# A sliding-window matmul on one core: loading the fp32 weights by hardware DMA in 8 KB rows and casting them on VectorE

## The chip, the cores and the metric

The kernel runs on one core of one Trainium2 chip. The metric is device time in microseconds (us), lower is better. A profile of one execution goes with each kernel. Its span (first to last instruction) is 1.5 to 2 us shorter than the time of the run.

## The reference

```python
B, S, D, W = 4, 4096, 4096, 64      # x: [4, 4096, 4096] fp32, w: [4096, 4096] fp32
for b in range(B):
    o = int(offsets[b])             # known only at run time
    results.append(x[b, o:o+W] @ w) # [64, 4096] @ [4096, 4096]
```

So four windows of 64 rows, 256 rows in all, are multiplied by one big matrix. w is 67.1 MB and is read once. The windows of x are four times 1 MB. The output is 4.2 MB.

## The kernel before

The four windows are laid into two tiles of 128 partitions (two windows of 64 rows in each), transposed on TensorE, and used as stationary operands. w streams through in four groups of 1024 columns. GpSimd issues nearly all loads as software DMAs, which cast fp32 to fp16 on the way, 4 KB of each row of w at a time (1024 columns of fp32): on the page each of these loads of w writes 256.0 KB for 512 KB read.

```python
NG = 1024
wh_pool = ctx.enter_context(tc.tile_pool(name="wh", bufs=36))     # fp16 w tiles
xpair = [x_pool.tile([P, D], fp16, name=f"xpair{g}") for g in range(G)]
# ... three early loads by hardware DMA, eight by software DMA, then x:
for b in range(B):
    g, m = divmod(b, 2)
    nc.gpsimd.dma_start(                                   # casts to fp16
        out=xpair[g][m * WIN : (m + 1) * WIN, :],          # 64 partitions
        in_=x[b][bass.ds(off_vals[b], WIN), :],
    )
# ... then all other w tiles, by nc.gpsimd.dma_start(out=w_tile(ng, ki)[:], in_=w_src(ng, ki))
for ng in range(n_ng):                                     # 4 column groups
    for ki in range(n_full):
        for g in range(G):
            for j in range(n_sub):
                nc.tensor.matmul(out=acc[g][:, j * NT : (j + 1) * NT],
                                 lhsT=xT[g][:, ki * KT : (ki + 1) * KT],
                                 rhs=whk[:, j * NT : (j + 1) * NT], ...)
    # ... copy PSUM out, store
```

## Time and profile before

| | before |
|---|---|
| time, median of 3 runs | 188.69 us (188.68 to 189.26) |
| span of the profile | 187.1 us |
| PE / VectorE / ScalarE busy | 131.8 / 14.2 / 8.5 us |
| DMA | 9 tenths or more in all slices but the first and the last |
| HBM read / written | 71.30 / 4.19 MB |

These lines are from the page of the kernel before. PE is TensorE's matmuls, PEld its weight loads, DVE is VectorE, ACT ScalarE and POOL GpSimd. PE's line gives busy time, share of the span and instructions. The DMA and GB/s lines cut the span into 40 equal slices: the busy share of the DMA engines in tenths, and what they moved. GB/s counts the bytes written, so a load that casts to fp16 counts half of what it reads (the packets on the page come to 40.72 MB, for 71.30 MB read and 4.19 MB written in HBM).

```profile
span 187.1 us, 1496 instructions
PE 131.8 (70%) x576; PEld 54.8 (29%) x576; DVE 14.2 (8%) x13; ACT 8.5 (5%) x9; POOL 71.6 (38%) x140
...
DMA  4999999999999999999999999999999999999993
GB/s 147 291 205 218 215 205 209 210 209 210 210 208 210 262 209 262 208 209 209 210 209 209 209 210 210 209 209 210 210 209 208 211 208 210 209 209 210 258 416 154
...
HBM read 71.30 MB, written 4.19 MB: 403 GB/s over the span
```

The next lines are three pieces of the chain of waits (start in us, length in us, what). Each piece is one round of eight software loads: the ninth is issued when the first has landed.

```profile
82.21 9.48 DMA wh<-in_w_dram
...
92.23 9.50 DMA wh<-in_w_dram
...
102.26 9.48 DMA wh<-in_w_dram
```

From 92.23 to 102.26 is 10.03 us; over several rounds it is 10.02 us for eight loads of 524,288 bytes of fp32, so 418.5 GB/s are read. That is where the time goes: 75.5 MB at 418.5 GB/s would take 180.4 of the 187.1 us. PE waits for w again and again (22.5 us in all), and is not the limit.

These are GpSimd's issues of w loads from about 21 us on, each held until one of the four x loads had landed (columns: start, length, engine, line, operation, and in brackets the idle time before and what ended it).

```profile
21.10 0.53 POOL L112 DMA_DIRECT2D wh<-in_w_dram  x1 [1.97 <-DMA xpair<-in_x_dram]
...
23.53 0.53 POOL L112 DMA_DIRECT2D wh<-in_w_dram  x1 [1.90 <-DMA xpair<-in_x_dram]
25.93 0.53 POOL L112 DMA_DIRECT2D wh<-in_w_dram  x1 [1.88 <-DMA xpair<-in_x_dram]
...
28.37 0.53 POOL L112 DMA_DIRECT2D wh<-in_w_dram  x1 [1.92 <-DMA xpair<-in_x_dram]
```

One x load lands every 2.4 us. Each reads 1.05 MB, so x is read at about 430 GB/s, at full rate, and written as fp16 into 64 partitions at half of that, about 215 GB/s. (That is by the landings. The DMA's own count from 18.6 to 28.4 us is 210 GB/s written.)

### The profile page before, as it was taken

Reading aid. Unit: us, or ns where it says so; the run is one execution under the profiler, and the core shown is the slowest. Engines: PE = TensorE matmul, PEld = TensorE weight load, DVE = VectorE, ACT = ScalarE, POOL = GpSimd, SP = SyncE. Lnnn points to the kernel's source line nnn. Section 1 sums busy time; section 2 is a strip of 40 time slices with the busy share of each in tenths; the row PEclk is TensorE's granted clock in tenths of the full one; section 3 lists DMA queues with packets and bytes.
Section 4 is the critical chain, followed back from the end, with each engine's and each line's share of the span. In section 5 each row is a group of like instructions: output and inputs, shape, how many; then the busy total and the mean of one; then the engine's idle time right before and its main releaser. Section 6 shows DMA issues by size and latency. Waiting matters only on the chain.

```text
span 187.1 us, 1496 instructions
## 1 busy us (share of the span) xinstructions
PE 131.8 (70%) x576; PEld 54.8 (29%) x576; DVE 14.2 (8%) x13; ACT 8.5 (5%) x9; POOL 71.6 (38%) x140
## 2 busy tenths in 40 slices
PE   0000079999999585988888888888888888888820
PEld 0000076444444232333322322332233233323300
DVE  0000079100000020000002000000020000000020
ACT  2420000000002000000002000000020000000020
POOL 7343224343343242444344434434443426344200
PEclk9999999999999999699999999999999999999996
DMA  4999999999999999999999999999999999999993
GB/s 147 291 205 218 215 205 209 210 209 210 210 208 210 262 209 262 208 209 209 210 209 209 209 210 210 209 209 210 210 209 208 211 208 210 209 209 210 258 416 154
DMA packets 20344, 40.72 MB, mean 218 GB/s; under 512 B 2290, under 2 KB 2546, under 8 KB 20082
## 3 DMA queue, kind: packets, MB, share of 16 engines
q0 software_dynamic: 19040, 36.97, 102.2%
q1 hardware_dynamic: 866, 2.36, 3.3%
q10 hardware_dynamic: 432, 1.31, 2.1%
q8 instruction: 4, 0.07, 0.1%
q14 instruction: 2, 0.02, 0.0%
HBM read 71.30 MB, written 4.19 MB: 403 GB/s over the span
## 4 chain that ended last, share of the span: by engine, by line
DMA 64%; PE 17%; issue 7%; DVE 3%; POOL 3%; POOLq 1%; ACT 0%
DMA wh<-in_w_dram 57%; PE ps L146 16%; DMA xpair<-in_x_dram 6%; DVE xT L132 3%; POOL wh L74 2%; POOLq L83 1%; POOL wh L112 1%; PE ps L125 1%; PE ps L175 1%; DVE sth L188 0%; ACT sth L187 0%; POOLq L112 0%; POOL identity masks.py:197 0%; POOLq L94 0%; POOL xpair L94 0%
## 5 line engine op out<-in xcount | busy, mean ns | idle before, releaser
L146 PE MATMUL ps<-wh,xT 128*128 128x512 f16 x508 | 125.2, 382 | 22.6 <-DMA wh<-in_w_dram 22.5
L112 POOL DMA_DIRECT2D wh<-in_w_dram x116 | 61.2, 528 | 92.6 <-DMA wh<-in_w_dram 74.7
L146 PEld LDWEIGHTS <-xT 128*128 128x128 f16 x508 | 49.3, 97 | 98.2 <-issue 47.8
L125 PE MATMUL ps<-identity,xpair 128*128 128x128 f16 x64 | 5.5, 265 | 24.7 <-DMA xpair<-in_x_dram 24.7
L125 PEld LDWEIGHTS <-xpair 128*128 128x128 f16 x64 | 5.1, 123 | 24.9 <-issue 24.9
L132 DVE CAST xT<-ps 128x1024 f16<-128x1024 f32 x8 | 9.1, 1213 | 24.4 <-PE ps L125 24.4
L165 DVE COPY stage<-ps 128x1024 f32<-128x1024 f32 x2 | 2.4, 1224 | 70.9 <-PE ps L146 70.9
L164 ACT COPY stage<-ps 128x1024 f32<-128x1024 f32 x2 | 2.0, 1012 | 79.0 <-PE ps L146 79.0
L74 POOL DMA_DIRECT2D wh<-in_w_dram x8 | 4.4, 586 | 0.8 <-POOLq L211 0.8
L188 DVE COPY sth<-ps 128x512 f32<-128x512 f32 x2 | 1.4, 692 | 38.5 <-PE ps L175 38.5
L94 POOL DMA_DIRECT2D xpair<-in_x_dram x4 | 2.1, 519 | 5.7 <-DMA wh<-in_w_dram 5.7
L160 DVE COPY stage<-ps 128x1024 f32<-128x1024 f32 x1 | 1.2, 1223 | 32.2 <-DMA out_dram<-stage 32.2
L167 POOL DMA_DIRECT2D out_dram<-stage x4 | 2.1, 533 | 3.1 <-DMA wh<-in_w_dram 3.1
L79 ACT CAST wh<-w 128x1024 f16<-128x1024 f32 x3 | 3.0, 1043 | 4.7 <-DMA w<-in_w_dram 4.7
L159 ACT COPY stage<-ps 128x1024 f32<-128x1024 f32 x1 | 1.0, 1012 | 47.3 <-PE ps L146 47.3
L187 ACT COPY sth<-ps 128x512 f32<-128x512 f32 x2 | 1.2, 586 | 38.9 <-PE ps L175 38.9
L175 PE MATMUL ps<-whl,xT 128*128 128x512 f16 x4 | 1.3, 378 | 0.5 <-ACT sth L187 0.5
L107 POOL DMA_DIRECT2D whl<-in_w_dram x2 | 1.1, 528 | 1.3 <-DMA wh<-in_w_dram 1.3
L79 ACT ACT_TABLE_LOAD x1 | 1.3, 1283 | 1.3 <-PEq L211 1.3
L175 PEld LDWEIGHTS <-xT 128*128 128x128 f16 x4 | 0.4, 97 | 1.1 <-issue 0.4
masks.py:199 POOL TENSOR_SCALAR_AFFINE_SELECT identity<-identity 128x128 f16<-128x128 f16 x1 | 0.3, 287 | 0.1
masks.py:197 POOL MEMSET identity<- 128x128 f16 x1 | 0.3, 295 | 0.0
(4 smaller groups left out, 0.4 us busy)
## 6 DMA issues: line engine op xcount, KB each, us to landing
wh<-in_w_dram POOLq DMA_DIRECT2D x124, 256.0 KB, 9.5
xpair<-in_x_dram POOLq DMA_DIRECT2D x4, 512.0 KB, 12.7
out_dram<-stage POOLq DMA_DIRECT2D x4, 512.0 KB, 8.3
w<-in_w_dram SPq DMA_DIRECT2D x2, 512.0 KB, 6.4
out_dram<-sth SPq DMA_DIRECT2D x3, 256.0 KB, 5.6
w<-in_w_dram ACTq DMA_DIRECT2D x1, 512.0 KB, 4.3
out_dram<-stage SPq DMA_DIRECT2D x1, 512.0 KB, 7.0
out_dram<-stage ACTq DMA_DIRECT2D x1, 512.0 KB, 7.1
```

The lines of the kernel that those rows point to most:

```text
L74: nc.gpsimd.dma_start(out=w_tile(0, ki)[:], in_=w_src(0, ki))
L79: nc.scalar.copy(out=w_tile(0, k)[:], in_=w32[k][:])
L83: nc.values_load(off_i32[0:1, 2 * b : 2 * b + 1], engines=[POOL], min_val=0, max_val=S - WIN,)
L94: nc.gpsimd.dma_start(out=xpair[g][m * WIN : (m + 1) * WIN, :], in_=x[b][bass.ds(off_vals[b], WIN), :],)
L112: nc.gpsimd.dma_start(out=w_tile(ng, ki)[:], in_=w_src(ng, ki))
L125: nc.tensor.matmul(out=ps[t][:, q * KT : (q + 1) * KT], lhsT=xpair[g][:, k * KT : (k + 1) * KT], rhs=identity[:], start=True, stop=True,)
L132: nc.vector.tensor_copy(out=xT[g][:, t * NG : (t + 1) * NG], in_=ps[t][:])
L146: nc.tensor.matmul(out=acc[g][:, j * NT : (j + 1) * NT], lhsT=xT[g][:, ki * KT : (ki + 1) * KT], rhs=whk[:, j * NT : (j + 1) * NT], start= ...
L164: nc.scalar.copy(out=stage[(ng, 0)][:], in_=acc[0][:])
L165: nc.vector.tensor_copy(out=stage[(ng, 1)][:], in_=acc[1][:])
L167: nc.gpsimd.dma_start(out=out[2 * g : 2 * g + 2, :, cs : cs + NG], in_=stage[(ng, g)][:],)
L175: nc.tensor.matmul(out=acc[g][:, j * NT : (j + 1) * NT], lhsT=xT[g][:, ki * KT : (ki + 1) * KT], rhs=wlast[j][:], start=False, stop=True,)
```

## The change

The intent: no software DMAs at all. w is loaded as fp32 by the sync engine's hardware DMAs in 1 MB pieces with rows of 8 KB, and cast to fp16 on VectorE, which is nearly idle. Two column groups of 2048 take the place of four of 1024. The hardware loads of this kernel write fp32 tiles, so x too is loaded as fp32, two windows by the scalar engine's queue and two by the sync engine's, and cast afterwards.

The diff, cut to its core:

```diff
-    NG = 1024
+    NG = 2048
-    wh_pool = ctx.enter_context(tc.tile_pool(name="wh", bufs=36))
+    wf_pool = ctx.enter_context(tc.tile_pool(name="wf", bufs=8))
+    wh_pool = ctx.enter_context(tc.tile_pool(name="wh", bufs=8))
     sth_pool = ctx.enter_context(tc.tile_pool(name="sth", bufs=4))
+    def load(ng, ki):
+        t = wf_pool.tile([P, NG], fp32, name="wf", tag="wf")
+        nc.sync.dma_start(out=t[:], in_=w[ki * P : (ki + 1) * P, ng * NG : (ng + 1) * NG])
+        return t
+    def cast(f):
+        t = wh_pool.tile([P, NG], fp16, name="wh", tag="wh")
+        nc.vector.tensor_copy(out=t[:], in_=f[:])
+        return t
+    wf[(0, 0)] = load(0, 0)
+    q = [nc.scalar, nc.sync]
+    qe = [ACT, SP]
+    for g in range(G):
+        for m in range(2):
+            b = 2 * g + m
+            o = nc.values_load(off_i32[0:1, 2 * b : 2 * b + 1], engines=[qe[m]], ...)
-        nc.gpsimd.dma_start(
-            out=xpair[g][m * WIN : (m + 1) * WIN, :],
-            in_=x[b][bass.ds(off_vals[b], WIN), :],
+            q[m].dma_start(
+                out=x32[g][m * WIN : (m + 1) * WIN, :],
+                in_=x[b][bass.ds(o, WIN), :],
             )
     # ... (cut) all other w loads on nc.sync; x cast half by VectorE, half by ScalarE;
     # ... transposes in 8 PSUM banks; the same 512 matmuls; the first column group's
     # ... output (2 MB) is stored after the last w load, the second's in 8 tiles
```

More of the change, by code (lines that the diff above doesn't have):

```diff
@@ L26 @@
     P = 128
-    KT = 128
     NT = 512
-    NG = 1024
-    n_k = D // KT
+    NG = 2048
+    n_k = D // P
     n_ng = N // NG
@@ L33 @@
     G = B // 2
-    POOL = mybir.EngineType.Pool
+    SP = mybir.EngineType.SP
+    ACT = mybir.EngineType.Activation
     const_pool = ctx.enter_context(tc.tile_pool(name="const", bufs=1))
     x_pool = ctx.enter_context(tc.tile_pool(name="xp", bufs=1))
-    wh_pool = ctx.enter_context(tc.tile_pool(name="wh", bufs=36))
-    w32_pool = ctx.enter_context(tc.tile_pool(name="w32", bufs=1))
-    whh_pool = ctx.enter_context(tc.tile_pool(name="whh", bufs=2))
+    wf_pool = ctx.enter_context(tc.tile_pool(name="wf", bufs=8))
+    wh_pool = ctx.enter_context(tc.tile_pool(name="wh", bufs=8))
+    wl_pool = ctx.enter_context(tc.tile_pool(name="wl", bufs=4))
     st_pool = ctx.enter_context(tc.tile_pool(name="st", bufs=1))
@@ L46 @@
     identity = const_pool.tile([P, P], fp16, name="identity")
-    off_t = const_pool.tile([1, B], mybir.dt.int64, name="off_t")
-    xpair = [x_pool.tile([P, D], fp16, name=f"xpair{g}") for g in range(G)]
+    x32 = [x_pool.tile([P, D], fp32, name=f"xrow{g}") for g in range(G)]
+    x16 = [x_pool.tile([P, D], fp16, name=f"xhalf{g}") for g in range(G)]
     xT = [x_pool.tile([P, D], fp16, name=f"xT{g}") for g in range(G)]
-    ps = [psum_pool.tile([P, NG], fp32, name=f"ps{t}") for t in range(4)]
@@ L54 @@
-    wh_tiles = {}
-    def w_tile(ng, ki):
+    ps = [psum_pool.tile([P, NT], fp32, name=f"bank{t}") for t in range(8)]
+    off_i32 = offsets[None, :].bitcast(mybir.dt.int32)
+    ctx.enter_context(tc.manual_schedule())
+    def load(ng, ki):
[3 more added lines that the diff above has]
+    def cast(f):
         t = wh_pool.tile([P, NG], fp16, name="wh", tag="wh")
-        wh_tiles[(ng, ki)] = t
+        nc.vector.tensor_copy(out=t[:], in_=f[:])
@@ L59, in w_tile @@
         return t
-    def w_src(ng, ki):
-        return w[ki * KT : (ki + 1) * KT, ng * NG : (ng + 1) * NG]
-    N_EARLY = 3
-    early_q = [nc.sync, nc.scalar, nc.sync]
-    w32 = [w32_pool.tile([P, NG], fp32, name=f"w32_{k}") for k in range(N_EARLY)]
-    nc.sync.dma_start(out=off_t[:], in_=offsets[None, :])
-    for k in range(N_EARLY):
-        early_q[k].dma_start(out=w32[k][:], in_=w_src(0, k))
-    n_pre = 8
-    for ki in range(N_EARLY, N_EARLY + n_pre):
-        nc.gpsimd.dma_start(out=w_tile(0, ki)[:], in_=w_src(0, ki))
@@ L76 @@
-    make_identity(nc, identity[:])
-    for k in range(N_EARLY):
-        nc.scalar.copy(out=w_tile(0, k)[:], in_=w32[k][:])
-    off_i32 = off_t.bitcast(mybir.dt.int32)
-    off_vals = [
-        nc.values_load(
-            off_i32[0:1, 2 * b : 2 * b + 1],
-            engines=[POOL],
-            min_val=0,
-            max_val=S - WIN,
-        )
-        for b in range(B)
-    ]
-    for b in range(B):
-        g, m = divmod(b, 2)
-        nc.gpsimd.dma_start(
-            out=xpair[g][m * WIN : (m + 1) * WIN, :],
-            in_=x[b][bass.ds(off_vals[b], WIN), :],
-        )
@@ L99 @@
-    wlast = [
-        whh_pool.tile([P, NT], fp16, name="whl", tag="whl") for _ in range(n_sub)
-    ]
+    wf = {}
+    wf[(0, 0)] = load(0, 0)
+    make_identity(nc, identity[:])
+    q = [nc.scalar, nc.sync]
[3 more added lines that the diff above has]
+            b = 2 * g + m
+            o = nc.values_load(
+                off_i32[0:1, 2 * b : 2 * b + 1],
+                engines=[qe[m]],
+                min_val=0,
+                max_val=S - WIN,
+                skip_runtime_bounds_check_because="offsets are drawn below S - WIN",
+            )
+            q[m].dma_start(
+                out=x32[g][m * WIN : (m + 1) * WIN, :],
+                in_=x[b][bass.ds(o, WIN), :],
+            )
@@ L102 @@
+    wlast = []
     for ng in range(n_ng):
-        for ki in range(N_EARLY + n_pre if ng == 0 else 0, n_k):
+        for ki in range(n_k):
+            if (ng, ki) == (0, 0):
+                continue
             if ng == n_ng - 1 and ki == n_k - 1:
@@ L106 @@
                     cs = ng * NG + j * NT
-                    nc.gpsimd.dma_start(
-                        out=wlast[j][:],
-                        in_=w[ki * KT : (ki + 1) * KT, cs : cs + NT],
-                    )
-            else:
-                nc.gpsimd.dma_start(out=w_tile(ng, ki)[:], in_=w_src(ng, ki))
-    stage = {}
-    for ng in (1, 2):
-        for g in range(G):
-            stage[(ng, g)] = st_pool.tile(
-                [P, NG], fp32, name=f"stage{ng}{g}", tag=f"stage{ng}{g}"
-            )
-    for g in range(G):
-        for t in range(4):
-            for q in range(8):
-                k = 8 * t + q
+                    t = wl_pool.tile([P, NT], fp32, name="wl", tag="wl")
+                    nc.sync.dma_start(out=t[:], in_=w[ki * P : (ki + 1) * P, cs : cs + NT])
+                    wlast.append(t)
+            else:
+                wf[(ng, ki)] = load(ng, ki)
+    wh = {(0, 0): cast(wf[(0, 0)])}
+    H = D // 2
+    for g in range(G):
+        nc.vector.tensor_copy(out=x16[g][:, :H], in_=x32[g][:, :H])
+        nc.scalar.copy(out=x16[g][:, H:], in_=x32[g][:, H:])
+        for t in range(8):
+            for i in range(4):
+                k = 4 * t + i
                 nc.tensor.matmul(
-                    out=ps[t][:, q * KT : (q + 1) * KT],
-                    lhsT=xpair[g][:, k * KT : (k + 1) * KT],
+                    out=ps[t][:, i * P : (i + 1) * P],
+                    lhsT=x16[g][:, k * P : (k + 1) * P],
                     rhs=identity[:],
@@ L131, with mm @@
                 )
-            nc.vector.tensor_copy(
-                out=xT[g][:, t * NG : (t + 1) * NG], in_=ps[t][:]
-            )
+            dst = xT[g][:, t * NT : (t + 1) * NT]
+            if t % 2 == 0:
+                nc.vector.tensor_copy(out=dst, in_=ps[t][:])
+            else:
+                nc.scalar.copy(out=dst, in_=ps[t][:])
+    def mm(g, j, ki, rhs, start, stop):
+        nc.tensor.matmul(
+            out=ps[4 * g + j][:],
+            lhsT=xT[g][:, ki * P : (ki + 1) * P],
+            rhs=rhs,
+            start=start,
+            stop=stop,
+        )
@@ L136 @@
+    stage = [st_pool.tile([P, NG], fp32, name=f"stage{g}") for g in range(G)]
     for ng in range(n_ng):
-        par = ng % 2
-        acc = [ps[2 * par], ps[2 * par + 1]]
         last = ng == n_ng - 1
-        cs = ng * NG
-        n_full = n_k - 1 if last else n_k
-        for ki in range(n_full):
-            whk = wh_tiles[(ng, ki)]
+        for ki in range(n_k - 1 if last else n_k):
+            if (ng, ki) not in wh:
+                wh[(ng, ki)] = cast(wf[(ng, ki)])
             for g in range(G):
@@ L145 @@
                 for j in range(n_sub):
-                    nc.tensor.matmul(
-                        out=acc[g][:, j * NT : (j + 1) * NT],
-                        lhsT=xT[g][:, ki * KT : (ki + 1) * KT],
-                        rhs=whk[:, j * NT : (j + 1) * NT],
-                        start=(ki == 0),
-                        stop=(ki == n_k - 1),
-                    )
-        if not last:
-            if ng == 0:
-                st0 = [
-                    st_pool.tile([P, NG], fp32, name=f"stage0{g}", tag="stage0")
-                    for g in range(G)
-                ]
-                nc.scalar.copy(out=st0[0][:], in_=acc[0][:])
-                nc.vector.tensor_copy(out=st0[1][:], in_=acc[1][:])
-                nc.sync.dma_start(out=out[0:2, :, cs : cs + NG], in_=st0[0][:])
-                nc.scalar.dma_start(out=out[2:4, :, cs : cs + NG], in_=st0[1][:])
-            else:
-                nc.scalar.copy(out=stage[(ng, 0)][:], in_=acc[0][:])
-                nc.vector.tensor_copy(out=stage[(ng, 1)][:], in_=acc[1][:])
-                for g in range(G):
-                    nc.gpsimd.dma_start(
-                        out=out[2 * g : 2 * g + 2, :, cs : cs + NG],
-                        in_=stage[(ng, g)][:],
-                    )
-        else:
-            ki = n_k - 1
@@ L173 @@
+                    mm(g, j, ki, wh[(ng, ki)][:, j * NT : (j + 1) * NT], ki == 0, ki == n_k - 1)
+        if not last:
             for j in range(n_sub):
                 for g in range(G):
-                    nc.tensor.matmul(
-                        out=acc[g][:, j * NT : (j + 1) * NT],
-                        lhsT=xT[g][:, ki * KT : (ki + 1) * KT],
-                        rhs=wlast[j][:],
-                        start=False,
-                        stop=True,
-                    )
-                hs = cs + j * NT
@@ L183 @@
-                sth = [
-                    sth_pool.tile([P, NT], fp32, name="sth", tag="sth")
-                    for _ in range(G)
-                ]
-                nc.scalar.copy(out=sth[0][:], in_=acc[0][:, j * NT : (j + 1) * NT])
-                nc.vector.tensor_copy(
-                    out=sth[1][:], in_=acc[1][:, j * NT : (j + 1) * NT]
-                )
-                if j == 0:
-                    nc.sync.dma_start(out=out[0:2, :, hs : hs + NT], in_=sth[0][:])
-                    nc.sync.dma_start(out=out[2:4, :, hs : hs + NT], in_=sth[1][:])
-                else:
-                    nc.scalar.dma_start(out=out[0:2, :, hs : hs + NT], in_=sth[0][:])
-                    nc.sync.dma_start(out=out[2:4, :, hs : hs + NT], in_=sth[1][:])
+                    dst = stage[g][:, j * NT : (j + 1) * NT]
@@ new lines, with cast_last @@
+                    if g == 0:
+                        nc.scalar.copy(out=dst, in_=ps[4 * g + j][:])
+                    else:
+                        nc.vector.tensor_copy(out=dst, in_=ps[4 * g + j][:])
+    for g in range(G):
+        nc.sync.dma_start(out=out[2 * g : 2 * g + 2, :, 0:NG], in_=stage[g][:])
+    ki = n_k - 1
+    def cast_last(j):
+        t = wl_pool.tile([P, NT], fp16, name="wlh", tag="wlh")
+        nc.vector.tensor_copy(out=t[:], in_=wlast[j][:])
+        return t
+    wlh = [cast_last(0)]
@@ new lines @@
+    for j in range(n_sub):
+        if j + 1 < n_sub:
+            wlh.append(cast_last(j + 1))
+        cs = (n_ng - 1) * NG + j * NT
+        for g in range(G):
+            mm(g, j, ki, wlh[j][:], False, True)
+            s = sth_pool.tile([P, NT], fp32, name="sth", tag="sth")
+            if g == 0:
+                nc.scalar.copy(out=s[:], in_=ps[4 * g + j][:])
+            else:
+                nc.vector.tensor_copy(out=s[:], in_=ps[4 * g + j][:])
+            q[g].dma_start(out=out[2 * g : 2 * g + 2, :, cs : cs + NT], in_=s[:])
```

## The prediction

> **What bounds the kernel now.** The DMA engines. Part 2 of the page shows DMA at 9 tenths in every slice from the second to the last but one. The chain of waits is a row of pieces of about 10.0 us: eight 512 KB (fp32 side) loads per 10.02 us = 418.5 GB/s read from HBM. (The page's 209 GB/s counts the fp16 side of the casting loads.) 71.3 MB read and 4.19 MB written, 75.5 MB, at 418.5 GB/s take 180.4 of the 187.1 us span. The rest is start (first bytes after about 2 us, not full until 4.5) and end (data thins out at about 184.3, span ends 187.1). PE is busy 131.8 us (70%); it waits for w 22.5 us, in steps of about 0.2; VectorE (14.2) and ScalarE (8.5) idle. GpSimd waits for earlier loads to land: issuing is not the limit either.
>
> **What the change does.** The bytes in HBM stay the same (75.5 MB); the cast moves from the DMA to VectorE. So it is worth only what hardware fp32 loads with 8 KB rows run faster or slower than 418.5 GB/s, plus both ends.
>
> Added on VectorE: 63 casts of 128x2048 and 4 small. The PSUM casts in the trace (1213 ns for 1024 columns, 692 for 512) give a slope of 1.02 ns per column, so at most about 2.26 us each (estimate). [...] Either is below the 2.5 us in which 1 MB arrives, so casts hide; eight 1 MB buffers are 20 us of slack over the x transposes and the middle eviction (4 copies, 2.8 us).
> PE does the same 512 matmuls, starting near 20 us, not 30.2, which buys nothing.
>
> **Rate.** [...] This trace has no stretch of hardware loads alone: mixed, 410 GB/s at 4.5 to 5.0 us; the stores at 178 to 181 us ran at 421. I take 423, i.e. 1.9 us less over 75.5 MB.
>
> **Ends.** Start: offset reads precede the x loads and w loads 1 to 7; 0.5 to 1 us lost. End: 4.19 MB of stores come after the last w load (now 3.1), at DMA rate; but four staging tiles are reused, and VectorE's third must wait for a store queued behind the two 1 MB ones: about 1 us of idle DMA. Together +1.5 us, off the 1.9 gained.
>
> **Prediction.** Time minus span is 1.6 us before; I keep it. 187.4 us, 8 in 10 between 183.3 and 192.0. Faster by over 2%: 0.24; within 2%: 0.64; slower by over 2%: 0.12.
>
> **What would show it.** DMA full from about 3 us to the end; GB/s in middle slices 415 to 430 (now fp32 on both sides); [...] PE waiting on VectorE casts in steps of about 0.5 us; a dip in GB/s in the last two or three slices.
>
> **What would make it wrong.** Hardware loads with 8 KB rows near 432 GB/s or more (then about 184 or less, faster), or 408 or less (then 192 or more, slower); x loads into 64 partitions at half rate (up to 2.5 us); casts at 2.3 us with hand-offs that make VectorE the limit; a longer gap in the last stores.

The sum is 187.4 us: 188.69, less 1.9 for the rate, plus 1.5 for the ends (these add up to 188.3; see the slip of arithmetic below). The 423 GB/s stands as the estimate, which the trace before does not show: beside it are that trace's 410 GB/s (mixed loads) and 421 (stores).

## More of the kernel before

The main comparison has its own runs of the kernel before (188.97 us). The experiments came in three jobs on three chips. Each job timed the kernel before again on its own chip (188.75, 188.78 and 188.97 us), and each ratio is taken within one job.

## The result

The changed kernel takes 197.55 us (median of 4, 197.18 to 197.66) against 188.97 us for the kernel before (median of 4). The ratio is 1.0454, with a 95% interval of 1.0435 to 1.0472: 4.5% slower. Ratios in the experiments come out as ratios of mean times without each kernel's first run, so they are not quite the ratios of the medians quoted.

The same lines of the page after the change. All loads are fp32 now, so the GB/s line counts what is read as well.

```profile
span 195.7 us, 1538 instructions
PE 128.0 (65%) x576; PEld 56.3 (29%) x576; DVE 91.3 (47%) x85; ACT 14.0 (7%) x19; POOL 0.7 (0%) x6
...
DMA  6999999999999999999999999999999999999975
GB/s 214 228 218 224 214 385 424 415 419 427 425 415 422 424 427 412 422 424 427 415 419 422 425 420 417 420 425 425 417 422 424 422 415 422 424 422 401 433 280 212
...
L62 DVE CAST wh<-wf 128x2048 f16<-128x2048 f32 x63 | 77.1, 1227 | 79.1 <-DMA wf<-in_w_dram 79.0
```

The DMA line is the trap: DMA is busy at 9 tenths nearly throughout, as predicted. The GB/s line under it splits the run into two stretches. In slices 1 to 5 (0 to 24.5 us) only 214 to 228 GB/s move. In slices 7 to 36 it is 412 to 427. The casts are 1227 ns each, well under the 2.26 us of the prediction's upper estimate.

The next lines are windows of the same trace: start and end, length, busy time of PE, weight load, VectorE, ScalarE and GpSimd with counts, and last the granted clock, the DMA's busy share and GB/s.

```profile
7.00:10.00 3.00, 0.00 (x0) 0.00 (x0) 1.22 (x1) 0.00 (x0) 0.00 (x0) 1.00 0.97 202
10.00:15.00 5.00, 0.00 (x0) 0.00 (x0) 0.00 (x0) 0.00 (x0) 0.00 (x0) 1.00 0.99 213
15.00:19.00 4.00, 0.00 (x0) 0.00 (x0) 0.01 (x1) 0.04 (x1) 0.00 (x0) 1.00 1.03 233
19.00:22.00 3.00, 1.73 (x16) 1.62 (x16) 2.13 (x3) 2.99 (x2) 0.00 (x0) 1.00 0.97 229
...
40.00:175.00 135.00, 102.38 (x432) 42.17 (x432) 68.78 (x59) 2.05 (x4) 0.00 (x0) 0.99 1.01 421
```

The middle runs at 421 GB/s; I had predicted 423. The slow stretch is the time in which the four x loads are under way: they are issued between 3 and 9 us, and the casts of the second pair start at 26 us. 4.19 MB of x at 215 GB/s take 19.5 us, at 421 GB/s 10.0 us. That would be 9.5 us, a little more than the whole loss.

The last stores show a smaller loss. Copies into staging tiles wait for earlier stores to land, and the last two slices fall to 280 and 212 GB/s:

```profile
189.36 0.59 ACT L164 COPY sth<-bank 128x512 f32<-128x512 f32 x1 [3.03 <-DMA out_dram<-sth]
...
190.80 1.29 DVE L166 COPY sth<-bank 128x512 f32<-128x512 f32 x2 [3.89 <-DMA out_dram<-sth]
```

### The profile page after: what moved, and what is told of

The parts are those of the page before. It is cut to its first block, busy times and chain, and to the rows that moved or that the text cites. A ratio compares the mean times of both kernels' runs of the same rounds, so it can differ in the third digit from the quotient of the medians. Undisturbed runs are those within 1.5% of the kernel's fastest.

```text
span 195.7 us, 1538 instructions
## 1 busy us (share of the span) xinstructions
PE 128.0 (65%) x576; PEld 56.3 (29%) x576; DVE 91.3 (47%) x85; ACT 14.0 (7%) x19; POOL 0.7 (0%) x6
## 3 DMA queue, kind: packets, MB, share of 16 engines
HBM read 71.30 MB, written 4.19 MB: 386 GB/s over the span
## 4 chain that ended last, share of the span: by engine, by line
DMA 88%; DVE 5%; SPq 2%; ACT 1%; PE 1%; issue 1%; ACTq 0%; DVEq 0%
DMA wf<-in_w_dram 78%; DMA xrow<-in_x_dram 7%; DVE wh L62 5%; DMA out_dram<-sth 3%; SPq L73 2%; ACT sth L164 1%; PE bank L121 1%; SPq L57 0%; ACTq L167 0%; DVEq L62 0%; SPq L80 0%; ACTq L164 0%
## 5 line engine op out<-in xcount | busy, mean ns | idle before, releaser
L121 PE MATMUL bank<-wh,xT 128*128 128x512 f16 x504 | 119.1, 382 | 35.1 <-DVE wh L62 35.1
L62 DVE CAST wh<-wf 128x2048 f16<-128x2048 f32 x63 | 77.1, 1227 | 79.1 <-DMA wf<-in_w_dram 79.0
L107 PE MATMUL bank<-identity,xhalf 128*128 128x128 f16 x64 | 7.1, 303 | 23.5 <-DVE xhalf L102 23.4
L107 PEld LDWEIGHTS <-xhalf 128*128 128x128 f16 x64 | 6.3, 142 | 24.0 <-DVE xhalf L102 23.7
L102 DVE CAST xhalf<-xrow 128x2048 f16<-128x2048 f32 x2 | 2.5, 1228 | 12.3 <-DMA xrow<-in_x_dram 12.3
L116 DVE CAST xT<-bank 128x512 f16<-128x512 f32 x8 | 5.5, 692 | 2.3 <-PE bank L107 2.2
L166 DVE COPY sth<-bank 128x512 f32<-128x512 f32 x4 | 2.7, 687 | 5.6 <-DMA out_dram<-sth 3.9
L118 ACT CAST xT<-bank 128x512 f16<-128x512 f32 x8 | 4.6, 586 | 1.4 <-PE bank L107 1.2
L103 ACT CAST xhalf<-xrow 128x2048 f16<-128x2048 f32 x2 | 3.8, 1898 | 1.2 <-DMA xrow<-in_x_dram 1.2
L145 DVE COPY stage<-bank 128x512 f32<-128x512 f32 x4 | 2.5, 684 | 1.3 <-PE bank L121 1.3
```

The source lines that it names most:

```text
L62: nc.vector.tensor_copy(out=t[:], in_=f[:])
L102: nc.vector.tensor_copy(out=x16[g][:, :H], in_=x32[g][:, :H])
L103: nc.scalar.copy(out=x16[g][:, H:], in_=x32[g][:, H:])
L107: nc.tensor.matmul(out=ps[t][:, i * P : (i + 1) * P], lhsT=x16[g][:, k * P : (k + 1) * P], rhs=identity[:], start=True, stop=True,)
L116: nc.vector.tensor_copy(out=dst, in_=ps[t][:])
L118: nc.scalar.copy(out=dst, in_=ps[t][:])
```

## The experiments

**Theory P:** a fp32 load into a tile of 64 neighbouring partitions runs at half rate, because those partitions can't take more, and a load to the other 64 in flight at the same time doesn't help. **Rivals:** Q, two queues or offsets from registers slow the x loads; R, rows of 16 KB are slow; S, any load of 64 rows or 64 partitions is slow wherever the rows go; and the null, that the loss lies in the w loads or the casts, not in x.

All kernels of this section gave correct results.

### x over 128 partitions (x128)

A window of 64 rows of 16 KB is contiguous in HBM, so it can as well be read as 128 rows of 8 KB. Queues, offsets and bytes stay; the transposes pick the rows apart by a permuted identity.

```diff
-                out=x32[g][m * WIN : (m + 1) * WIN, :],
-                in_=x[b][bass.ds(o, WIN), :],
+                out=x32[b][:],                       # [128, 2048] fp32
+                in_=x[b][bass.ds(o, WIN), :].rearrange("r (h c) -> (r h) c", h=2),
...
+                    rhs=ident_h[:, h, :],            # identity "p (r h) -> p h r"
```

> Changed kernel, but each window of x is read as 128 rows of 8 KB into 128 partitions (same bytes, same two queues, same register offsets; the transposes pick rows apart again). Theory P (a fp32 load into 64 partitions runs at half rate, 215 GB/s against 421): all four x loads now run at about 420 GB/s, 9.5 us come back, about 188 us, and DMA moves over 400 GB/s from about 4 us on. Rival Q (x loads are slow because two queues or offsets from registers are used): still near 197.5 us, GB/s near 215 to about 25 us. Rival R (16 KB rows are slow): also 188 us, since the rows are halved here too; the next run tells it from P.

Measured: 189.77 us, ratio 1.003 (0.999 to 1.007). The loss is gone. The GB/s line of its page:

```profile
GB/s 206 352 347 393 426 419 426 420 426 422 417 420 420 422 424 420 422 424 422 413 420 422 420 419 429 420 422 417 420 422 422 419 424 422 422 419 401 419 277 219
```

Slices 2 to 4 are at 347 to 393 rather than 218 to 228. Q falls, for the two queues and the register offsets were kept. The time is 1.8 us above the 188 that I expected, and DMA was over 400 GB/s only from slice 5 on, not from 4 us. In part that is the start, which still isn't full: the sync engine issued its second x load only at 11.1 us and the next w load behind it at 11.5 (mending the start in x128_best, below, is worth 0.8 to 0.9 us; the rest is less than the 1.4 us by which the runs of x128 differ). These are pieces of its chain of waits (SPq is the sync engine's own instructions; L73 reads the offsets from HBM):

```profile
5.03 4.51 SPq L73
9.63 1.27 SPq L73
...
11.08 0.34 SPq L80
...
11.47 0.43 SPq L57
```

### 64 partitions with rows of 8 KB (x64_8k)

x128 also halved the rows of x. This run halves them and leaves the 64 partitions.

```diff
+            for h in range(2):
                 q[m].dma_start(
-                    out=x32[g][m * WIN : (m + 1) * WIN, :],
+                    out=x32[g][m * WIN : (m + 1) * WIN, h * 2048 : (h + 1) * 2048],
-                    in_=x[b][bass.ds(o, WIN), :],
+                    in_=x[b][bass.ds(o, WIN), h * 2048 : (h + 1) * 2048],
```

> Changed kernel, each x load cut into two column halves (64 partitions, 8 KB rows, eight DMAs). Theory P: still slow, 196.5 to 199 us, about 215 GB/s until 25 us. Rival R (16 KB rows are the cause): x at about 420 GB/s, about 188 us.

Measured: 197.18 us (one run).

```profile
GB/s 211 225 215 235 228 405 420 420 425 416 425 423 426 416 421 421 418 425 420 426 410 426 425 418 418 423 426 416 423 423 420 423 418 426 416 426 399 432 293 204
```

Still 211 to 235 GB/s in slices 1 to 5. R falls.

### 64 rows into every second partition (x64_step2)

This separates P from S. The load has 64 rows of 16 KB and writes 64 partitions, as in the changed kernel, but those of one window are 0, 2, ... 126 and those of the other 1, 3, ... 127.

```diff
-                out=x32[g][m * WIN : (m + 1) * WIN, :],
+                out=x32[g][m::2, :],
...
-                    rhs=identity[:],
+                    rhs=ident_m,                     # identity "p (r m) -> p m r"
```

> Changed kernel, but the 64 rows of a window go to every second partition (0, 2, ... 126 for one of a pair, 1, 3, ... 127 for the other), with 16 KB rows as before; the transposes pick the rows apart. Theory P1 (which partitions are written decides[...]): x faster than 215 GB/s, 188 to 195 us[...]. Rival P2 (a load of 64 rows or 64 partitions is slow wherever they lie): 196.5 to 198 us.

Measured: 189.67 us (one run).

```profile
GB/s 204 396 366 286 422 426 422 426 419 426 420 420 426 419 424 419 420 422 420 417 424 426 420 417 422 420 419 426 422 424 420 420 420 420 422 420 408 422 303 217
```

The half rate is gone, although each load still writes only 64 partitions: slices 2 and 3 are at 396 and 366, against 228 and 218. The window from 7 to 10 us, with x loads in flight on both queues, has 415 GB/s here, against 202 in the changed kernel (shown above):

```profile
7.00:10.00 3.00, 0.00 (x0) 0.00 (x0) 0.19 (x1) 0.00 (x0) 0.00 (x0) 1.00 1.02 415
```

(Slice 4, with 286, is in part short of work: from 13 to 16 us DMA is busy for 0.88, at 292 GB/s, and from 16 to 19 us for 0.81, at 279. Over its busy time alone that is about 330 to 345 GB/s (estimate), much like the 325 to 352 of x128 from 7 to 16 us; I didn't take apart why.) So what counts here is which partitions are written. S falls. Why neighbouring partitions are slow, no run here shows.

### w in two halves (x128_whalves)

If P holds it must hold for w as well. Each 1 MB load of w is cut into a load of partitions 0 to 63 and one of 64 to 127, in turn on the same queue.

```diff
-        nc.sync.dma_start(out=t[:], in_=w[ki * P : (ki + 1) * P, ng * NG : (ng + 1) * NG])
+        for h in range(2):
+            r = ki * P + h * 64
+            nc.sync.dma_start(out=t[h * 64 : (h + 1) * 64, :],
+                              in_=w[r : r + 64, ng * NG : (ng + 1) * NG])
```

> x128 with each w load cut into two 64-partition loads, low half and high half in turn on the same queue. Theory P (fp32 into 64 partitions runs at half rate, and a load of the other half behind it does not fill the other half): the whole stream at about 215 GB/s, 325 to 345 us. Rival (the two halves overlap, so that what slows x is something of the x loads, such as their source or their two queues): 189 to 195 us.

Measured: 326.0 us (one run; its granted clock was 0.798, but PE waits 124 us for w here and is not the limit). This is the window from 60 to 160 us:

```profile
60.00:160.00 100.00, 56.66 (x175) 20.48 (x173) 25.76 (x21) 0.00 (x0) 0.00 (x0) 0.77 1.02 224
```

The whole stream of w runs at 224 GB/s. With the load of the other half next in the queue, that is still only 0.53 of the 421 of x128. This also answers a doubt that the x loads leave: their two halves sat on two different queues, here they sit on one, and the rate is nearly the same. Nor is it the size of the loads, 512 KB: x128_rows4k, below, also loads w in pieces of 512 KB, over 128 partitions, and runs at 409 GB/s.

### Only the x loads changed, in the kernel before (before_hwx)

```diff
-        nc.gpsimd.dma_start(
-            out=xpair[g][m * WIN : (m + 1) * WIN, :],
+        (nc.sync if m else nc.scalar).dma_start(
+            out=x32[g][m * WIN : (m + 1) * WIN, :],
```

with casts of the two halves by VectorE and ScalarE, and the offsets read by the sync and scalar engines.

> The kernel before with only its x loads changed: fp32 into 64 partitions by hardware DMAs of the sync and scalar engines, cast by VectorE and ScalarE. Theory P: this part alone makes the kernel slower, by at most the 9.5 us, less where w loads of the other queue fill the DMA meanwhile: 191 to 198.5 us. If x loads aren't the cause (the loss would then lie in the w loads or the casts): 188 to 189.5 us.

Measured: 197.86 us, ratio 1.0472 (1.0454 to 1.0490). This part alone costs as much as the whole change does, even though nearly all of w still comes by software DMA on another queue. Those loads don't fill the gap: from 10 to 22 us 218 to 236 GB/s move (software loads counted at half), and the first eight of them took 13.0 to 31.4 us to land (median 28.8), against 7.5 to 13.1 (median 10.6) in the kernel before. Its GB/s line:

```profile
GB/s 172 309 227 219 228 199 208 209 209 209 211 208 209 210 259 232 239 209 209 211 208 209 209 209 210 208 210 210 208 210 247 224 211 208 259 213 209 210 259 214
```

The scheduler also moved the two small loads of the last tile of w earlier (to 14.5 and 133.6 us), which does not change the bytes. The null falls.

### x by software DMA, w by hardware (sw_x, then sw_x2)

sw_x gives x back to GpSimd's casting DMA and leaves w as changed.

```diff
-                engines=[qe[m]],
+                engines=[mybir.EngineType.Pool],
...
-            q[m].dma_start(
-                out=x32[g][m * WIN : (m + 1) * WIN, :],
+            nc.gpsimd.dma_start(
+                out=x16[g][m * WIN : (m + 1) * WIN, :],
```

> Changed kernel with the x loads given back to the software DMA, which casts and so writes half the bytes into the same 64 partitions; w stays as it is. Theory P, in the form that the bytes written into the 64 partitions set the rate: x reads run at full rate, 186.5 to 189 us. Rival S (any DMA of 64 partitions is slow, whatever it writes): still 195 us or more.

Measured: 193.05 us, ratio 1.0236: better than the changed kernel, but outside what I expected, and between the two theories' ranges. The trace shows one reason. GpSimd issues its four x loads at 5.7, 13.1, 18.7 and 23.4 us (it reads the offsets from HBM between them), x is late, VectorE's casts of w stand behind x in program order, and the eight buffers fill up. DMA then stands idle (windows as above; the last two figures are busy share and GB/s; "issue" is idle time in which the profile shows nothing waited for):

```profile
13.13 0.51 POOL L79 DMA_DIRECT2D xhalf<-in_x_dram  x1 [6.77 <-issue]
```

```profile
34.00:36.00 2.00, 2.00 (x21) 1.98 (x19) 1.68 (x3) 1.27 (x3) 0.00 (x0) 1.00 1.01 422
36.00:38.00 2.00, 2.00 (x10) 0.76 (x7) 2.00 (x3) 0.58 (x1) 0.00 (x0) 1.00 0.14 57
```

sw_x2 removes that: the offsets are loaded into SBUF by one small DMA and read from there, three w loads go ahead of x, and eight staging tiles are used at the end.

> sw_x with x early: offsets from SBUF behind one small DMA, three w loads ahead, eight staging tiles. Theory (sw_x missed its 188 us because GpSimd's offset reads took 5 to 7 us each, x came late, and with eight w buffers full the DMA stood idle from 36 to 39 us; 64 partitions written as fp16 are not slow themselves): 186 to 188.5 us, no idle DMA before the end. If 64 partitions are slow in themselves: 191 us or more.

Measured: 189.52 us, ratio 1.0041 (1.0000 to 1.0085). The idle DMA is gone, but this misses my range by 1 us. It is also 2.5 us above x128_best, below, which has the same start and end (these two ran in different jobs; by the ratios it is 1.4%). From 7 to 25 us the GB/s line, with x counted at half, adds up to at most 370 GB/s read (my estimate from the windows of that run: 4.57 MB written in 18 us, plus at most the 2.1 MB of x that the cast drops). So casting loads into 64 partitions, beside hardware loads of w, come near full rate without reaching it (at most 370 of 421 GB/s). At 370 rather than 421 GB/s these 18 us lose 2.2 us (estimate), so nearly all of the 2.5 us lies there. I made no run that tells why.

### Rows of 4 KB (x128_rows4k)

This run tests the step of the prediction about the rate: the same 1 MB tiles of w, each as two loads of 4 KB rows.

```diff
+        for h in range(2):
+            cs = ng * NG + h * 1024
-        nc.sync.dma_start(out=t[:], in_=w[ki * P : (ki + 1) * P, ng * NG : (ng + 1) * NG])
+            nc.sync.dma_start(out=t[:, h * 1024 : (h + 1) * 1024],
+                              in_=w[ki * P : (ki + 1) * P, cs : cs + 1024])
```

> x128 with each 1 MB load of w cut into two loads of 1024 columns, so 4 KB rows and 512 KB each. [...] If row length doesn't matter at this size: 189 to 190.5 us.

Measured: 195.05 us, ratio 1.0331 (1.0311 to 1.0351), 5.3 us more than x128 (another job; 3% by the ratios). That is far outside the 189 to 190.5 us of "row length doesn't matter". The first fence is the window from 40 to 165 us of x128_rows4k, the second the same window of x128:

```profile
40.00:165.00 125.00, 91.66 (x392) 37.76 (x391) 62.42 (x53) 2.05 (x4) 0.00 (x0) 1.00 1.03 409
```

```profile
40.00:165.00 125.00, 95.33 (x402) 39.28 (x402) 64.06 (x55) 2.05 (x4) 0.00 (x0) 0.99 1.01 421
```

409 against 421 GB/s. Cutting the loads halved the rows and the size of each load together, so this run does not part the two. It does part hardware from software DMAs: the kernel before also loads 4 KB rows in pieces of 512 KB of fp32, and reads 418.5 GB/s. With equal pieces the casting software DMA of these kernels is the faster one; the hardware DMA makes up for it with 8 KB rows and 1 MB pieces.

### Both ends mended (x128_sth8, x128_best)

x128_sth8 is x128 with eight staging tiles for the last row of output in place of four:

```diff
-    sth_pool = ctx.enter_context(tc.tile_pool(name="sth", bufs=4))
+    sth_pool = ctx.enter_context(tc.tile_pool(name="sth", bufs=8))
```

> x over 128 partitions, and eight staging tiles of the last row in place of four. Theory (the last stores wait for staging tiles to come free: DMA at 277 and 219 GB/s in the last two slices of the x128 run): the two stretches of idle DMA at the end go, 1.5 to 2.5 us less than x128, so 187.0 to 188.3 us. Rival (the end is held by the latency of the last casts, matmuls and copies): less than 0.5 us changes.

Measured: 187.88 us, ratio 0.9943 (0.9922 to 0.9964). As expected.

x128_best also reads the offsets from SBUF and puts three w loads in front of that read:

```diff
+    nc.sync.dma_start(out=off_t[:], in_=offsets[None, :])
+    N_FIRST = 3
+    for ki in range(N_FIRST):
+        wf[(0, ki)] = load(0, ki)
```

> As x128_sth8, and the offsets are read from SBUF behind one small DMA, with three w loads issued ahead of it, so that the DMA has work while offsets are read. Theory: DMA is full from about 2 us on (in x128 it moved 325 to 350 GB/s from 7 to 16 us and less before 4 us), another 1.5 to 2.5 us: 185 to 186.5 us, 1.2 to 2% faster than the kernel before. If the start does not matter: as x128_sth8.

Measured: 186.97 us (5 runs, 186.83 to 187.18), ratio 0.9902 (0.9887 to 0.9916). The GB/s line is now full from the second slice:

```profile
GB/s 164 422 429 424 422 421 419 422 419 421 417 424 424 422 421 424 419 424 419 421 415 421 424 421 422 422 422 419 419 424 422 421 417 424 424 424 393 430 388 175
```

The start gained 0.9 us, less than the 1.5 to 2.5 expected, so the time is half a microsecond above the range. This version beats both kernels, by 1% and by about 5%. It is within 2% of the kernel before: the rate in the middle is 421 against 418.5 GB/s, and the bytes are the same.

## Why the prediction was wrong

The prediction said 187.4 us, with 64% on "within 2%". Measured: 197.55 us, outside the range.

**What was right.** DMA bounds both kernels. The rate of hardware loads in 8 KB rows was predicted at 423 GB/s and is 421; it is worth 1.1 us over 75.5 MB, not 1.9. (The trace before had no stretch of hardware loads alone to take 423 from, so that it came this close is in part luck.) The casts were expected to hide even at 2.26 us. They take 1227 ns and are hidden (VectorE waits 79 us for w). The start and the end lose something: predicted 1.5 us together; mending them gained 1.6 us at the end and 0.8 us at the start, by the ratios of x128, x128_sth8 and x128_best. Against the kernel before, x128 is 0.6 us slower although its rate is worth 1.1 us, so its ends cost about 1.7 us (estimate).

**What failed.** The step is the term "x loads into 64 partitions at half rate (up to 2.5 us)". The prediction put it among the things that would make it wrong, outside the sum, and mis-sized it: 2.5 us is about what one such load of 1.05 MB loses (4.9 us at 215 GB/s, 2.5 at 421), and there are four. The record gives only the size, not the reasoning: I took it that a load to partitions 0 to 63 on one queue and one to 64 to 127 on the other would together run at full rate. They don't. While x loads were in flight on both queues, 202 to 233 GB/s moved, and one after the other on one queue it was 224. So all four x loads ran at half rate. The estimate for that is 9.5 us; the ratio falls from 1.0454 to 1.003 when it is taken away (x128), 8 us. None of the runs timed a fp32 load of one half alone.

**Why the kernel before did not show it.** Its x loads go to 64 partitions as well, and land every 2.4 us at full read rate. But they cast, so they write 215 GB/s while reading 430: they write at about the rate that the fp32 loads into 64 partitions show. The change doubled the bytes written into the same partitions. That both sides of this come to about 215 GB/s (210 to 215 and 202 to 233) is measured; that the software DMA would be limited there too if it did not cast was not tried.

**A slip of arithmetic.** The prediction's own terms (188.69, less 1.9, plus 1.5) add up to 188.3 us, not 187.4. The measured time is far from both.

**What the page could not tell.** The signature named in the prediction, "DMA full from about 3 us to the end", came true in the busy line and was no use: a transfer that is held up keeps the DMA busy (0.97 to 1.03 from 7 to 22 us, at 202 to 233 GB/s). The GB/s line shows it.

**What stays open.** Why loads to opposite halves, in flight at once on two queues, do not fill each other's gaps was not tested; all the runs show is that they don't. Why sw_x2 stays 2.5 us above x128_best is open too.

## What to carry to other kernels

When a cast moves out of a DMA, look at the bytes written and at which partitions they go to, not only at the bytes read (x64_step2 writes as many bytes per partition as the changed kernel, and is fast): fp32 loads into tiles of 64 neighbouring partitions moved about 215 GB/s in all here (202 to 233 measured), half of the 421 of loads into 128, although loads to both halves were in flight. Reshape the load so that it spans all 128 partitions (more, shorter rows, or every second partition) and let a permuted identity in the transpose put the rows right; that cost nothing visible here (x128 took 189.77 us against 197.55), as TensorE is not the limit (busy 65% of the span of the changed kernel). Read the GB/s line beside the DMA's busy line, for a slowed transfer looked busy here (0.97 to 1.03); and where DMA bounds both kernels at nearly the same rate, as here at 418.5 and 421 GB/s, look at the small odd loads (8 us here) and the ends of the run (1.6 and 0.8 us).
